# A first part whose weights, vectors, taps and x are laid out by the host

## The chip, the cores and the metric

The kernel runs on one core of a Trainium2 chip. The metric is the device time of one execution in microseconds; before the change the median of three runs is 2349.42 us (2344.43 to 2352.29). The core has five engines that run side by side and meet at semaphores: PE (TensorE, matmuls and transposes, with its weight loads listed as PEld), DVE (VectorE), ACT (ScalarE), POOL (GpSimd) and SP (SyncE, which here only issues DMAs). Sixteen DMA engines move data between HBM and the on-chip memory (SBUF, 128 partitions). Matmul results go to PSUM.

## The reference

A decoder trunk of two layers on x of 256 tokens by 2048 features in float32. Layer 0 mixes tokens by a Conformer convolution module, layer 1 by differential attention; each layer ends with a squared-ReLU MLP. All is modulated by a vector c through six vectors per layer (shift, scale and gate for the mixer and for the MLP):

```python
cond = jax.nn.silu(c)
mod = cond @ ada_w[i] + ada_b[i]
sh_m, sc_m, g_m, sh_f, sc_f, g_f = [m[:, None, :] for m in jnp.split(mod, 6, axis=-1)]
h = x * (1.0 + sc_m) + sh_m
# layer 0
u = h @ w1 + b1
a, gt = jnp.split(u, 2, axis=-1)
u = a * jax.nn.sigmoid(gt)
u = depthwise_causal_conv(u, w_dw, width=31) + b_dw
y = jax.nn.silu(layer_norm(u, g, b)) @ w2 + b2
# every layer
x = layer_norm(DEEPNORM_ALPHA * x + g_m * y, ln_mix_g[i], ln_mix_b[i])
h = x * (1.0 + sc_f) + sh_f
y = jnp.square(jax.nn.relu(h @ mlp_w1 + mlp_b1)) @ mlp_w2 + mlp_b2
x = layer_norm(DEEPNORM_ALPHA * x + g_f * y, ln_ffn_g[i], ln_ffn_b[i])
```

## The kernel before

Every product with weights is made of three matmuls: a weight and an activation are each split into a high part (a cast to fp32r, on ACT) and a low part (the rest, a subtraction on DVE), and high by high, low by high and high by low are summed in PSUM (L580 to L582 in the first part, L669 to L672 in the rest). A weight block is 1 MB, 128 partitions by 2048 columns (`w_pw` or `w_w`); its two halves are split one after the other into `wh` and `wl` (L568 and L569, L629 and L631).

The first part, to which the change is confined, runs from the start to the second pointwise product of the convolution module, some 465 us in. It computes h and its first product (pw1, 2048 by 4096) while the modulation vectors are still being made. The 16 blocks of 128 features are taken in six slices (`SLICES`: 1, 1, 2, 4, 4, 4). For each slice the scale and shift are computed first (the ada weights of the slice, 32-column matmuls on PE, L327 and L290, or multiply-adds on DVE, L249), then h of the slice is made, and then PE takes the slice's share of pw1 for eight groups of output columns, with the sums kept in SBUF (`sums`, `vtok`, L1118 to L1122). While PE works on a slice, the ada work of the next one runs between its matmuls. Behind the last slice come the gated unit, the depthwise convolution on PE (`cv`, L896), and the remaining modulation vectors of layer 0.

Weights and vectors are read as the reference holds them:

- An ada block is a strip of 128 to 1024 columns out of rows of 12288, for 2 to 16 row blocks (L208 to L220, L306 to L321). A row of a piece is 512 bytes in the first slices and 1, 2 or 4 KB later. For the first three slices scale and shift stand side by side in one block, which takes two loads.
- A pw1 block is loaded as two halves (the value columns and the gate columns), with rows of 4 KB or 2 KB (L549 to L559).
- x is read with tokens on partitions into `z`, in four pieces (`X_AT`). For h it must have features on partitions: PE transposes it (`h_t`, L508 and L1090), DVE and ACT read the transposed block from PSUM, multiply and add (`h_h`, L517, L520, L1095), and then split it (`h_hi`, `h_lo`). For two blocks at a time both read one PSUM tile; DVE makes one, ACT the other. When two pairs of a slice are done, ACT multiplies z in place by ALPHA (L1080), eight times in all, since the residual of the layer needs ALPHA times x.
- Small vectors (c, biases, layer norm factors) are read as rows of 128 (`rows_c`, `rows_adab`, `small_rows`, 18 loads), transposed on PE and copied to SBUF as columns (`as_cols`, L129 to L137). The taps of the depthwise convolution are transposed too and spread into `wct` by 4 copies on DVE and 12 on ACT (L976, L978).

The order of PE is written out for the whole program, that of DVE, ACT and SP for the first part (`manual_schedule`); each engine takes its instructions in that order. SP issues every load except one. It waits until the buffer is free and until one of eight semaphores is (a load reuses that of the eighth load before it). The buffers of ada blocks are reused in turn (`ada_raw`: two of their own, and pieces of `conv_ux` and `conv_x` that the convolution needs later); the four of pw1 blocks are `raw`.

Of the kernel before, what the change touches and what calls it, by code (L numbers as in the profile page):

```python
# [76 lines left out]

@with_exitstack
def trunk(
# [41 lines left out]
    def load_rows(rows_list, name, queue=None):  # L121

        rt = work.tile([P, P], F32, tag="S", name=f"rows_{name}", bufs=3)
        o = 0
        for r in rows_list:
            (queue or nc.scalar).dma_start(rt[o:o + r.shape[0], :], r)
            o += r.shape[0]
        return rt[:o, :]

    def as_cols(rt, name):  # L130

        n = rt.shape[0]
        pt = tp_tile(f"pt_{name}")
        nc.tensor.transpose(out=pt[:, :n], in_=rt, identity=ident[:n, :n])
        ct = const.tile([P, n], F32, name=f"cols_{name}")
        nc.vector.tensor_copy(ct, pt[:, :n])
        return ct  # L137

    def vec_rows(v):
        return v.rearrange("(n p) -> n p", p=P)  # L140
# [5 lines left out]
    taps = work.tile([P, NG], F32, tag="C", name="taps")[:4 * CW]  # L146
    small_rows = {}
    rows_sb = work.tile([P, NG], F32, tag="bc_b2", name="small_rows", bufs=1)

    def load_small(n, name, vs):  # L150
        o = 0
        for v in vs:
            r = vec_rows(v)
            nc.sync.dma_start(rows_sb[o:o + r.shape[0], n * P:(n + 1) * P], r)
            o += r.shape[0]
        small_rows[name] = rows_sb[:o, n * P:(n + 1) * P]

    cT = as_cols(c_rows, "c")
# [51 lines left out]
    def slice_tiles(i, v, f0, nf):  # L210

        n0, w = (v * KC + f0) * P, nf * P
        per = 2048 // w
        av = ada_w[i].rearrange("(kc p) n -> p kc n", p=P)

        def load(a):
            t = ada_raw(f"aw_{i}_{v}_{f0}_{a}")
# [1 line left out]
            nc.sync.dma_start(tv, av[:, per * a:per * (a + 1), n0:n0 + w])
# [84 lines left out]
    def ada_both_steps(i, f0, nf, ms):  # L304
# [6 lines left out]
        av = ada_w[i].rearrange("(kc p) n -> p kc n", p=P)  # L311

        def load(b, k=None):
            t = ada_raw(f"aw_{i}_b{k}_{f0}_{b}")
            tv = t.rearrange("p (j n) -> p j n", n=wt)
            for n, (v, _) in enumerate(ms):
                if k in (None, n):
                    n0 = (v * KC + f0) * P
# [1 line left out]
                    nc.sync.dma_start(tv[:, :, o:o + w], av[:, per * b:per * (b + 1), n0:n0 + w])  # L320
# [178 lines left out]
    def to_featT(src, pair, mul, add, name, c2s):  # L499


        pts = {}
        for c2 in c2s:
            pts[c2] = tp_tile(f"{name}_t{c2}")
            for j in range(2):
                cc = 2 * c2 + j
                for t in range(NT):
                    nc.tensor.transpose(out=pts[c2][:, j * S + t * P: j * S + (t + 1) * P],  # L508
                                        in_=src[:, t, cc * P:(cc + 1) * P], identity=ident)

# [589 lines left out]
    def put_h(s, c2, now=True):  # L1100
# [10 lines left out]
        if now:  # L1111
            rest()
# [728 lines left out]
```

## Time and profile before

| | |
|---|---|
| median of three runs | 2349.42 us (2344.43 to 2352.29) |
| span of the profiled execution, first to last instruction | 2342.9 us |
| instructions | 28838 |
| moved by DMA | 606.5 MB, mean 259 GB/s |
| mean granted clock of TensorE | 0.995 |
| matmuls of pw1 (L580 to L582) | 768 |
| ada blocks of layer 0 in the first part | 88 MB (5.25 of 6 vectors) |

The page gives no time of the profiled execution outside its span. In the views below a row of a timeline holds the start in us, the duration in us, the engine, the line, the operation, the tile it writes and the tiles it reads, the shape, a count and, in brackets, the idle time before it with what ended it. SPq and ACTq are issues of DMAs. A row of the groups holds the count, then the busy time in us with the mean of one in ns, and the idle time before. Matmul durations overlap, since PE is pipelined; what a matmul costs in a row of others is the distance between starts.

### The profile page before, as it was taken

The numbers are of one execution on the slowest core, as the hardware profiler recorded it, in microseconds if no ns is written. First come the engines' busy times: TensorE is split into PE (matmuls) and PEld (weight loads), VectorE is DVE, ScalarE is ACT, GpSimd is POOL, SyncE is SP. The second block draws the span as 40 slices with busy tenths as digits, with TensorE's granted clock in tenths as the row PEclk, the third lists the DMA queues.
The fourth block names the chain that finished last, engine by engine and source line by source line (L and its number), as shares of the span: only waits on it lengthen the run. The fifth ranks groups of instructions, "written<-read, shape, count | busy, mean of one in ns | idle before, by whom it ended". The sixth has DMA issues, their size and how long they took to land.

```text
span 2342.9 us, 28838 instructions
## 1 busy us (share of the span) xinstructions
PE 2279.1 (97%) x11265; PEld 1809.2 (77%) x11265; DVE 1743.6 (74%) x2031; ACT 1089.7 (47%) x1503; POOL 149.4 (6%) x110
## 2 busy tenths in 40 slices
PE   7999989999999999999999999999999999999999
PEld 4676647777788888888878888877888888888886
DVE  5787788878887888877878876887975655655566
ACT  3344674365345445445454454545443443443442
POOL 0000002002200000000004200010220000000000
PEclk9999999999999999999999999999999999999999
DMA  9998489869988888888847655784876565555563
GB/s 342 377 341 295 164 314 376 316 221 329 326 315 308 312 290 307 308 301 291 310 163 269 242 201 195 256 319 162 305 247 202 180 197 191 187 186 193 189 223 108
DMA packets 264721, 606.50 MB, mean 259 GB/s; under 512 B 11137, under 2 KB 24583, under 8 KB 251527
## 3 DMA queue, kind: packets, MB, share of 16 engines
q1 hardware_dynamic: 264472, 604.62, 73.9%
q8 instruction: 88, 1.44, 0.3%
q14 instruction: 49, 0.39, 0.0%
q10 hardware_dynamic: 112, 0.05, 0.0%
HBM read 602.48 MB, written 2.15 MB: 258 GB/s over the span
## 4 chain that ended last, share of the span: by engine, by line
PE 74%; issue 16%; DVE 6%; ACT 2%; DMA 2%; POOL 0%; POOLq 0%; ACTq 0%; DVEq 0%; SPq 0%
PE w_ps L669 18%; PE w_ps L671 18%; PE w_ps L672 18%; DVE wl_w L631 1%; DMA w_w<-in_mlp_w_dram 1%; PE pw_ps L669 1%; PE qkv_v_ps L672 1%; PE qkv_v_ps L669 1%; PE qkv_v_ps L671 1%; PE qkv_q_ps L672 1%; PE qkv_q_ps L669 1%; DVE acc L379 1%; PE qkv_q_ps L671 1%; PE pw_ps L671 1%; PE pw_ps L672 1%
## 5 line engine op out<-in xcount | busy, mean ns | idle before, releaser
L631 DVE TENSOR_TENSOR wl_w<-w_w,wh_w 128x1024 fp32r<-128x1024 f32 x510 | 633.3, 1259 | 340.0 <-ACT wh_w L629 339.3
L629 ACT CAST wh_w<-w_w 128x1024 fp32r<-128x1024 f32 x512 | 537.0, 1054 | 703.4 <-PE w_ps L672 563.9
L669 PE MATMUL w_ps<-wh_w,hm_hi 128*128 128x512 f32 x1024 | 402.3, 393 | 3.0 <-ACT hm_hi L490 3.0
L671 PE MATMUL w_ps<-wl_w,u_hi 128*128 128x512 f32 x1024 | 399.4, 390 | 4.1 <-DVE wl_w L631 4.1
L671 PE MATMUL w_ps<-wl_w,hm_hi 128*128 128x512 f32 x1024 | 399.5, 390 | 2.5 <-DVE wl_w L631 2.5
L672 PE MATMUL w_ps<-wh_w,hm_lo 128*128 128x512 f32 x1024 | 399.3, 390 | 1.6 <-DVE hm_lo L493 1.6
L669 PE MATMUL w_ps<-wh_w,u_hi 128*128 128x512 f32 x1024 | 400.6, 391 | 0.0
L672 PE MATMUL w_ps<-wh_w,u_lo 128*128 128x512 f32 x1024 | 399.1, 390 | 0.0
L379 DVE SCALAR_TENSOR_TENSOR acc<-adaw,cond,acc 128x2048 f32<-128x2048 f32 (+1 forms) x105 | 244.5, 2329 | 0.1
L669 PEld LDWEIGHTS w_ps<-wh_w,hm_hi 128*128 128x128 f32 x1024 | 192.5, 188 | 47.5 <-ACT hm_hi L490 4.5
L671 PEld LDWEIGHTS w_ps<-wl_w,u_hi 128*128 128x128 f32 x1024 | 192.4, 188 | 45.3 <-DVE wl_w L631 5.8
L671 PEld LDWEIGHTS w_ps<-wl_w,hm_hi 128*128 128x128 f32 x1024 | 192.5, 188 | 43.4 <-DVE wl_w L631 4.6
L672 PEld LDWEIGHTS w_ps<-wh_w,hm_lo 128*128 128x128 f32 x1024 | 192.4, 188 | 43.0 <-DVE hm_lo L493 3.1
L669 PEld LDWEIGHTS w_ps<-wh_w,u_hi 128*128 128x128 f32 x1024 | 192.6, 188 | 42.0 <-issue 1.7
L672 PEld LDWEIGHTS w_ps<-wh_w,u_lo 128*128 128x128 f32 x1024 | 192.5, 188 | 40.2
L580 PE MATMUL pw_ps<-wh_pw,h_hi 128*128 128x512 f32 x256 | 105.7, 413 | 9.4 <-DVE sums L1122 3.3
L581 PE MATMUL pw_ps<-wl_pw,h_hi 128*128 128x512 f32 x256 | 101.5, 397 | 5.1 <-DVE wl_pw L569 5.1
L582 PE MATMUL pw_ps<-wh_pw,h_lo 128*128 128x512 f32 x256 | 100.8, 394 | 0.0
L569 DVE TENSOR_TENSOR wl_pw<-w_pw,wh_pw 128x1024 fp32r<-128x1024 f32 x64 | 77.5, 1220 | 21.2 <-ACT wh_pw L568 21.2
L568 ACT CAST wh_pw<-w_pw 128x1024 fp32r<-128x1024 f32 x64 | 65.8, 1050 | 41.6 <-PE pw_ps L582 24.5
L580 PEld LDWEIGHTS pw_ps<-wh_pw,h_hi 128*128 128x128 f32 x256 | 48.5, 190 | 39.5 <-issue 16.1
L581 PEld LDWEIGHTS pw_ps<-wl_pw,h_hi 128*128 128x128 f32 x256 | 48.7, 190 | 15.9 <-DVE wl_pw L569 7.2
(375 smaller groups left out, 3147.4 us busy)
## 6 DMA issues: line engine op xcount, KB each, us to landing
w_w<-in_mlp_w_dram SPq DMA_DIRECT2D x256, 1024.0 KB, 5.4
adaw<-in_ada_w_dram SPq DMA_DIRECT2D x96, 1024.0 KB, 5.6
aw<-in_ada_w_dram SPq DMA_DIRECT2D x40, 1024.0 KB, 7.3
w_pw<-in_conv_pw_w_dram SPq DMA_DIRECT2D x64, 512.0 KB, 9.1
conv_ux<-in_ada_w_dram SPq DMA_DIRECT2D x17, 1024.0 KB, 12.9
w_pw<-in_conv_pw_w_dram SPq DMA_DIRECT2D x16, 1024.0 KB, 9.2
w_qkv_q<-in_attn_qkv_w_dram SPq DMA_DIRECT2D x16, 1024.0 KB, 5.4
w_qkv_k<-in_attn_qkv_w_dram SPq DMA_DIRECT2D x16, 1024.0 KB, 5.2
```

Of the source, the lines that this page charges most:

```text
L379: nc.vector.scalar_tensor_tensor(st["acc"], w, cond[:, kc:kc + 1], st["acc"], ALU.mult, ALU.add)
L568: nc.scalar.copy(hq, rq)
L569: nc.vector.tensor_tensor(lq, rq, hq.bitcast(F32), op=ALU.subtract)
L580: nc.tensor.matmul(pss[t], lhsT=xh, rhs=wh, start=(kc == first), stop=False)
L581: nc.tensor.matmul(pss[t], lhsT=xh, rhs=wl, start=False, stop=False)
L582: nc.tensor.matmul(pss[t], lhsT=xl, rhs=wh, start=False, stop=(kc == last))
L629: nc.scalar.copy(hi, rq)
L631: eng.tensor_tensor(lo, rq, hi.bitcast(F32), op=ALU.subtract)
L669: nc.tensor.matmul(pss[tt], lhsT=xh, rhs=wh, start=(kc == 0 and job["bias"] is None), stop=False)
L671: nc.tensor.matmul(pss[tt], lhsT=xh, rhs=wl, start=False, stop=False)
L672: nc.tensor.matmul(pss[tt], lhsT=xl, rhs=wh, start=False, stop=(kc == nk - 1))
```

## The change

The host makes six new inputs (`lay_out`), and the first part reads them:

```diff
+def ada_specs():
+    out = []
+    for s, (f0, nf) in enumerate(SLICES):
+        if s < BOTH_PE and 2 * nf * P <= NG:
+            out += [("both", f0, nf, a) for a in range(2 * nf)]
+        else:
+            out += [(v, f0, nf, a) for v in (SC_M, SH_M) for a in range(nf)]
...
+def lay_out(inputs):
...
+        ada.append(aw[per * a:per * (a + 1), :, vs, f0:f0 + nf, :].transpose(1, 0, 2, 3, 4).reshape(P, 2048))
...
+    pw1 = [pw[c0:c0 + nk, :, :, g:g + ng].transpose(1, 0, 2, 3, 4).reshape(P, 2048)
+           for _, c0, nk, g, ng in pw1_specs()]
...
+        "x_t": i["x"][0].T.reshape(KC, P, S).transpose(1, 0, 2),
+        "taps_t": taps, "ada_tiles": np.stack(ada), "pw1_tiles": np.stack(pw1),
...
-    c_rows = load_rows([vec_rows(c[0])], "c", nc.sync)
-    adab0_rows = load_rows([vec_rows(ada_b[0])], "adab0")
+    vec0 = const.tile([P, KC + 6 * KC], F32, name="vec0")
+    nc.scalar.dma_start(vec0, cols_first)
+    vec1 = const.tile([P, cols_rest.shape[1]], F32, name="vec1")
...
+    xT = z.rearrange("p t (a n) -> p (t a) n", n=S)
...
             t = ada_raw(f"aw_{i}_{v}_{f0}_{a}")
-            tv = t.rearrange("p (j n) -> p j n", n=w)
-            nc.sync.dma_start(tv, av[:, per * a:per * (a + 1), n0:n0 + w])
-            return tv
+            nc.sync.dma_start(t, ada_tiles[ADA_AT[v, f0, nf, a]])
+            return t.rearrange("p (j n) -> p j n", n=w)
...
-                    nc.tensor.transpose(out=pts[c2][:, j * S + t * P: j * S + (t + 1) * P],
-                                        in_=src[:, t, cc * P:(cc + 1) * P], identity=ident)
...
+    def chunk_h(mul, add, c0, n):
+        h32 = [work.tile([P, 1, S], F32, tag="B", name=f"h0_h{c0 + j}") for j in range(n)]
+        for j in range(n):
+            cc = c0 + j
+            if j == 0:
+                nc.vector.tensor_scalar(h32[j][:, 0, :], xT[:, cc, :], mul[:, cc:cc + 1], add[:, cc:cc + 1],
+                                        ALU.mult, ALU.add)
+            else:
+                nc.scalar.activation(h32[j][:, 0, :], xT[:, cc, :], AF.Identity,
+                                     scale=mul[:, cc:cc + 1], bias=add[:, cc:cc + 1])
+        for j in range(n):
+            put_split(hT, c0 + j, 1, 0, S, h32[j])
...
-        for h in range(2):
-            raws["dma"] = nc.sync.dma_start(rv[:, :, h, :], src[:, :, h, :])
+        raws["dma"] = nc.sync.dma_start(raw, pw1_tiles[n])
...
         nc.vector.tensor_tensor(tmp, ps, gb[:, sl], op=ALU.mult)
-        nc.vector.tensor_tensor(z[:, t, sl], z[:, t, sl], tmp, op=ALU.add)
+        if times is None:
+            nc.vector.tensor_tensor(z[:, t, sl], z[:, t, sl], tmp, op=ALU.add)
+        else:
+            nc.vector.scalar_tensor_tensor(z[:, t, sl], z[:, t, sl], times, tmp, ALU.mult, ALU.add)
...
-    def alpha_x(q):
-        sl = slice(q * NG, (q + 1) * NG)
-        for t in range(NT):
-            nc.scalar.activation(z[:, t, sl], z[:, t, sl], AF.Copy, scale=ALPHA)
...
             if (s, h) == (3, 0):
-                load_small(0, "conv", [conv_pw1_b[0], conv_dw_b[0], conv_ln_g[0], conv_ln_b[0]])
-                nc.sync.dma_start(taps, conv_dw_w[0].rearrange("k (q c) -> (k q) c", q=4))
...
+                nc.sync.dma_start(vec1, cols_rest)
+                nc.sync.dma_start(wct.rearrange("p a k b -> p (a k b)"), taps_t)
+            elif (s, h) == (5, 9):
+                nc.sync.dma_start(z, x[0].rearrange("(t p) d -> p t d", p=P))
```

- Every ada block of layer 0 and every pw1 block is one load of 128 rows of 8 KB that lie together in HBM, in the order in which the kernel reads them.
- The vectors come as columns in two loads, `vec0` (c and layer 0's ada bias, on ACT's queue) and `vec1` (all others); the taps come as `wct` is used. Their transposes and copies are gone.
- x comes with features on partitions (`xT`, in the place of `z`, in the same four pieces), and h is made from it without a transpose. In slice 5 x is loaded once more, with tokens on partitions, into the same `z`. It isn't scaled by ALPHA there; the gated add of pw2 multiplies by it (`times`).

The order of all other instructions, and that of everything behind the first part, is the same on each engine. On SP the program begins before with (c's rows, ada blocks in halves, a piece of x, pw1 blocks in halves):

```order
L126 DMA rows_c<-in_c_dram 16x128
L320 DMA aw_bNone_0_139<-in_ada_w_dram 128x8x128 x2
L320 DMA aw_bNone_1_142<-in_ada_w_dram 128x8x128 x2
L1127 DMA z<-in_x_dram 128x2x256
L554 DMA w_pw_0_0_0_146<-in_conv_pw_w_dram 128x1024 x2
L554 DMA w_pw_4_0_0_149<-in_conv_pw_w_dram 128x1024 x2
L320 DMA conv_ux<-in_ada_w_dram 128x8x128 x4
```

and after the change with the same blocks, one load each:

```order
L338 DMA aw_bNone_0_132<-in_ada_tiles_dram 128x2048
L338 DMA aw_bNone_1_134<-in_ada_tiles_dram 128x2048
L1070 DMA z<-in_x_t_dram 128x512
L558 DMA w_pw_0_0_0_137<-in_pw_tiles_dram 128x2048
L558 DMA w_pw_4_0_0_139<-in_pw_tiles_dram 128x2048
L338 DMA conv_ux<-in_ada_tiles_dram 128x2048 x2
```

The blocks stand in the same order; c's load is no longer ahead of them.

On ACT, at the boundary to slice 2, before (one of two h blocks, the two casts, z's scaling, weight casts; brackets hold the semaphores that a row waits for):

```order
L520 ACTIVATE h_h_476<-h_t_454,mod_0_128,h_mul 128x256 [waits DVE_49,PE_49,Activation_49]
L490 CAST h_hi<-h_h_475 128x256
L490 CAST h_hi<-h_h_476 128x256 [waits Activation_49]
L1080 ACTIVATE z<-z 128x512 [waits DMAHW6_49,DMAHW1_49]
L1080 ACTIVATE z<-z 128x512
L568 CAST wh_pw_0_2_0_1_507<-w_pw_0_2_0_303 128x1024
```

and after:

```order
L526 ACTIVATE h_h_438<-z,mod_0_121,h_mul 128x256 [waits DMAHW5_49,DVE_49,Activation_49]
L508 CAST h_hi<-h_h_437 128x256 [waits DVE_49]
L508 CAST h_hi<-h_h_438 128x256 [waits Activation_49]
L572 CAST wh_pw_0_2_0_1_467<-w_pw_0_2_0_277 128x1024
L572 CAST wh_pw_2_2_0_0_486<-w_pw_2_2_0_279 128x1024 [waits DMAHW0_49,PE_49]
```

The two rows of scaling are gone, and the wait for DVE's block has moved from ACT's own h to the cast of DVE's h.

On SP, towards the end of slice 5, before (ada blocks of the vectors that are needed later):

```order
L219 DMA aw_2_8_3_1847<-in_ada_w_dram 128x4x512
L219 DMA aw_2_0_5_1901<-in_ada_w_dram 128x2x1024
L219 DMA aw_2_12_0_2010<-in_ada_w_dram 128x4x512
L219 DMA aw_2_0_6_2012<-in_ada_w_dram 128x2x1024
L219 DMA aw_2_12_1_2014<-in_ada_w_dram 128x4x512
```

and after:

```order
L243 DMA aw_2_8_3_1690<-in_ada_tiles_dram 128x2048
L243 DMA aw_2_0_5_1744<-in_ada_tiles_dram 128x2048
L1150 DMA z<-in_x_dram 128x2x2048
L243 DMA aw_2_12_0_1854<-in_ada_tiles_dram 128x2048
L243 DMA aw_2_0_6_1856<-in_ada_tiles_dram 128x2048
L243 DMA aw_2_12_1_1858<-in_ada_tiles_dram 128x2048
```

The load of x with tokens on partitions has come in, as one load of 2 MB.

More of the change, by code (lines that the diff above doesn't have):

```diff
@@ L119, in inv_sqrt @@
         nc.gpsimd.tensor_tensor(dst, src, neg_half.broadcast_to([P, n]), op=ALU.pow)
[L121 to L140, printed above, removed]
-    c_rows = load_rows([vec_rows(c[0])], "c", nc.sync)
-    adab0_rows = load_rows([vec_rows(ada_b[0])], "adab0")
-    vtok = big.tile([P, NT, D], F32, tag="uTl", name="vtok")
[L146 to L158, printed above, removed]
+    vec0 = const.tile([P, KC + 6 * KC], F32, name="vec0")
+    nc.scalar.dma_start(vec0, cols_first)
+    vec1 = const.tile([P, cols_rest.shape[1]], F32, name="vec1")
+    vtok = big.tile([P, NT, D], F32, tag="uTl", name="vtok")
+    cT = vec0[:, :KC]
     cond = const.tile([P, KC], F32, name="cond")
@@ L834, in base_bias, with add_gated @@
             defer(step * (q + 1), lambda q=q: quarter(q))
[L836 removed]
+    def add_gated(ps, gb, t, q, name, times=None):
         sl = slice(q * NG, (q + 1) * NG)
@@ L1084, in end_ada, with put_h @@
             f()
[L1086 to L1113 removed]
+    def put_h(s, c2):
+        f0, nf = SLICES[s]
+        c0, n = (f0, 1) if nf == 1 else (2 * c2, 2)
+        if c0 == f0:
+            nc.vector.tensor_scalar(mul[:, f0:f0 + nf], m_sc[:, f0:f0 + nf], 1.0, None, ALU.add)
+        chunk_h(mul, m_sh, c0, n)
     def add_up(g, s, pss):
@@ L1222, in trunk @@
                 split_half(s)
-            if s == 3 and 5 <= h < 9:
-                tap_columns(h - 5)
-            elif (s, h) == (3, 9):
-                conv_vectors()
+            if (s, h) == (3, 5):
+                nc.vector.tensor_reduce(eye, ident.rearrange("p (r c) -> p c r", c=32), axis=AX.X, op=ALU.add)
             if h in PAIR_AT[s]:
@@ L1335, in ln_t, with out_proj @@
         return [stats, norm]
-    def out_proj(pair, w2d, gate, name, pump, at_end, start=None, hold=False, on_pool=((),) * 4, bias=None):
+    def out_proj(pair, w2d, gate, name, pump, at_end, start=None, hold=False, on_pool=((),) * 4, bias=None,
+                 times=None):
         st = stats_tile(name)
@@ L1385, in trunk @@
     out_proj(lambda: oT, conv_pw2_w[0], gate0, "pw2", pump_t2, lambda st, t: ln_t(st, t, ALPHA, "lnm0"),
-             start=early_ve.__enter__, on_pool=POOL_T2,
+             start=early_ve.__enter__, on_pool=POOL_T2, times=ALPHA,
              bias=lambda q: lambda: [(bias0["one"][:, q:q + 1].broadcast_to([4, P]), bias0["hl"][:, n, :])
```

157 lines of the change are left out of this document (49 added, 108 removed).

## The prediction

> **What bounds the kernel now.** I read the page's head first, then the windows by stage, then the PE timeline of the first 260 us, since the change touches only that part.
>
> ```profile
> span 2342.9 us, 28838 instructions
> PE 2279.1 (97%) x11265; PEld 1809.2 (77%) x11265; DVE 1743.6 (74%) x2031; ACT 1089.7 (47%) x1503; POOL 149.4 (6%) x110
> ```
>
> PE is busy for 97% of the span. Matmul times overlap in this view, so that is not the last word, but it leaves at most some tens of microseconds of waits. Where they lie is seen by stage (columns: the busy time of PE, PEld, DVE, ACT and POOL with instructions, the granted clock, the DMA share, GB/s):
>
> ```profile
> 0.00:20.00 20.00, 8.16 (x43) 4.22 (x44) 5.58 (x14) 5.63 (x9) 2.02 (x12) 1.00 0.97 289
> 20.00:140.00 120.00, 111.26 (x576) 77.17 (x576) 87.91 (x137) 47.67 (x72) 0.00 (x0) 1.00 1.05 375
> 140.00:260.00 120.00, 114.04 (x665) 84.00 (x667) 96.85 (x142) 57.40 (x81) 0.00 (x0) 1.00 0.71 256
> 460.00:2342.00 1882.00, 1854.98 (x8405) 1516.14 (x8403) 1380.83 (x1485) 871.93 (x1180) 130.31 (x91) 1.00 0.71 244
> ```
>
> The reader is to see three stages. Until 140 us the DMA engines are full (shares 0.97 and 1.05) and PE has 20.6 us without work. From 140 to 260 the DMA has room (0.71) and PE lacks 6 us. From 460 on PE is short of 27 us in 1882; nothing there is touched, and the order of the instructions there is the same, so that part should only start earlier. So the first part has two bounds that lie close together: PE, and until 140 us the transfers.
>
> How fast the transfers go depends on the length of a row. The same view, in stretches in which the queue is full and nearly all pieces are alike: 512 bytes (2 to 10 us), 4 KB (24 to 28), 2 KB (60 to 68), half 8 KB (364 to 368), and layer 1's 8 KB rows among 2 KB ones (596 to 600, 700 to 712):
>
> ```profile
> 2.00:10.00 8.00, 2.55 (x18) 1.05 (x18) 0.94 (x4) 0.67 (x2) 0.58 (x3) 1.00 1.06 273
> 24.00:28.00 4.00, 4.00 (x37) 2.81 (x39) 2.07 (x3) 0.71 (x2) 0.00 (x0) 1.00 1.02 406
> 60.00:68.00 8.00, 8.00 (x49) 4.45 (x42) 4.64 (x6) 1.41 (x2) 0.00 (x0) 1.00 1.05 387
> 364.00:368.00 4.00, 4.00 (x30) 3.60 (x29) 1.00 (x2) 2.89 (x6) 0.00 (x0) 1.00 1.01 398
> 596.00:600.00 4.00, 4.00 (x19) 3.30 (x19) 0.00 (x0) 2.08 (x2) 0.00 (x0) 1.00 1.01 405
> 700.00:712.00 12.00, 12.00 (x58) 10.00 (x57) 9.42 (x7) 5.82 (x7) 0.00 (x0) 1.00 1.00 361
> ```
>
> So 512-byte rows cost a third of the rate (273 against 387 to 406), and from 2 KB on there is little left to win: 2 to 5%.
>
> **The start (edit 1: whole blocks, and c as a column).** The timelines of SP, PE and ACT:
>
> ```profile
> 1.17 4.18 SPq L320 DMA_DIRECT2D aw_bNone<-in_ada_w_dram  x4
> 7.45 1.94 PE L327 MATMUL aps_b<-aw_bNone,condr 128*32 128x256 f32 x16 [4.34 <-DMA aw_bNone<-in_ada_w_dram]
> 11.04 1.94 PE L327 MATMUL aps_b<-aw_bNone,condr 128*32 128x256 f32 x16 [1.65 <-DMA aw_bNone<-in_ada_w_dram]
> 15.88 2.93 ACT L568 CAST wh_pw<-w_pw 128x1024 fp32r<-128x1024 f32 x3
> 16.97 0.79 PE L580 MATMUL pw_ps<-wh_pw,h_hi 128*128 128x512 f32 x1 [2.39 <-ACT wh_pw L568]
> ```
>
> PE waits for the first 2 MB of ada weights; the second MB lands at about 10.9 us, 9.7 after the first issue at 1.17. 2.1 MB at 273 GB/s are 7.7 us, so 2.0 are latency. In the change SP issues these loads first, at about 0.7 (c's row load leaves SP), and 2.1 MB at 403 GB/s (the mean of 406, 398 and 405; the 361 is kept for the range) are 5.2 us: landed at 0.7 + 2.0 + 5.2 = 7.9, 3.0 us sooner. From there to the first conv matmul at 16.97 the chain stays (PE, ACT, PE, DVE, ACT); x and the first conv block follow in the queue (1.3 MB, 3.3 us, landed at 11.2), before ACT casts it at 15.88 - 3.0 = 12.9. With 0.1 from a shorter step in it: **3.1 us**; bounds 2.4 (at 361 GB/s) and 3.7 (less latency).
>
> **PE work that goes (edit 2: x, taps and vectors come with features on partitions).**
>
> ```profile
> 30.18 0.38 PE L1090 MATMUL h_t<-ident,z 128*128 128x128 f32 x2
> 30.40 0.38 PE L353 MATMUL apt_b<-ident,arow_b 128*128 128x128 f32 x2
> ```
>
> Two transposes hold PE for 0.22 us, so 0.11 each (the 0.38 is pipelined). 32 transposes of x go, of which the first 2 lie in the start's chain, and 9 for taps and vectors after the start. Until 140 us that is 14 + 5, **2.0 us**; from 140 to 260 it is 16 + 4, **2.2 us**. PE is the engine that is waited for in these places, so they count in full. The copies out of PSUM that go with them are small work of DVE and ACT.
>
> **Slice boundaries (edit 3: h is made from SBUF, and ACT no longer scales z by ALPHA).** The timelines of DVE and ACT at the boundary to slice 2:
>
> ```profile
> 50.50 0.54 DVE L517 TENSOR_SCALAR h_h<-h_t,h_mul,mod 128x256 f32<-128x256 f32 x1
> 52.05 0.76 DVE L493 TENSOR_TENSOR h_lo<-h_h,h_hi 128x256 fp32r<-128x256 f32 x2 [1.00 <-ACT h_hi L490]
> 51.16 0.56 ACT L520 ACTIVATE h_h<-h_t,mod,h_mul 128x256 f32<-128x256 f32 x1 [3.48 <-DVE h_h L517]
> 51.62 0.70 ACT L490 CAST h_hi<-h_h 128x256 fp32r<-128x256 f32 x2
> 52.22 1.15 ACT L1080 ACTIVATE z<-z 128x512 f32<-128x512 f32 x2
> 53.55 0.47 PE L580 MATMUL pw_ps<-wh_pw,h_hi 128*128 128x512 f32 x1 [2.27 <-DVE sums L1122]
> ```
>
> Both halves of a pair read one PSUM tile, and ACT starts its half only when DVE has ended its own (51.04, then 51.16). In the change ACT's half waits only for the factor, and the order rows show a wait of its own for the first cast; so both halves run beside each other, 0.6 us sooner per pair. DVE's own half shortens too:
>
> ```profile
> L247 DVE TENSOR_SCALAR aacc<-aw,cond 128x512 f32<-128x512 f32 x2 | 1.0, 480 | 0.0
> L517 DVE TENSOR_SCALAR h_h<-h_t,h_mul,mod 128x256 f32<-128x256 f32 x7 | 3.8, 542 | 3.3 <-PE h_t L508 3.2
> ```
>
> From SBUF twice the columns take 480 ns, from PSUM half take 542, so some 0.2 us more go. And four times 1.15 us of scaling leave ACT just ahead of a weight cast. There are 7 pairs. What counts are the waits of PE behind them: the 2.27 us at 53.55, and at the next three boundaries
>
> ```profile
> 88.72 0.50 PE L580 MATMUL pw_ps<-wh_pw,h_hi 128*128 128x512 f32 x1 [1.13 <-ACT h_hi L490]
> 93.44 0.50 PE L581 MATMUL pw_ps<-wl_pw,h_hi 128*128 128x512 f32 x1 [0.76 <-DVE wl_pw L569]
> 148.22 0.50 PE L581 MATMUL pw_ps<-wl_pw,h_hi 128*128 128x512 f32 x1 [1.66 <-DVE wl_pw L569]
> 206.24 0.50 PE L581 MATMUL pw_ps<-wl_pw,h_hi 128*128 128x512 f32 x1 [1.17 <-DVE wl_pw L569]
> ```
>
> These are 4.2 us until 140 and 2.8 after it. I take two thirds, **2.8 and 1.9 us**, since each wait follows one or two pairs of 0.8 us and a scaling; the bounds for both together are 1 (the DVE work between them sets the pace anyway) and 7 (all goes). The scaling comes back on DVE as a multiply inside the gated add, which takes a third operand:
>
> ```profile
> L249 DVE SCALAR_TENSOR_TENSOR aacc<-aw,cond,aacc 128x512 f32<-128x512 f32 x18 | 13.5, 750 | 0.4
> L840 DVE TENSOR_TENSOR z<-z,pw_g 128x512 f32<-128x512 f32 x7 | 4.8, 693 | 0.2
> ```
>
> That is 0.06 us eight times before 465 us; most of it lies beside PE's matmuls, and I count **0.2 us** lost for the last ones, ahead of the layer norm.
>
> **Transfers until 140 us.** Waits of PE that end with a DMA:
>
> ```profile
> 71.44 1.06 PE L327 MATMUL apsb<-conv_ux,condr 128*32 128x512 f32 x8 [1.49 <-DMA conv_ux<-in_ada_w_dram]
> 126.46 1.07 PE L290 MATMUL aps<-conv_ux,condr 128*32 128x512 f32 x8 [1.47 <-DMA conv_ux<-in_ada_w_dram]
> 360.47 1.08 PE L290 MATMUL aps<-aw,condr 128*32 128x512 f32 x4 [2.46 <-DMA aw<-in_ada_w_dram]
> ```
>
> The first two, **3.0 us**, go if the loads run ahead (bounds: none and both). The third stays: its load is issued when a buffer comes free, and rows of 4 KB become 8 KB there. By PE's side the stage gains 3.1 + 2.0 + 2.8 + 3.0 = 10.9 us. PE can't get ahead of its loads either: 289 x 20 + 375 x 120 is 50.8 MB by 140 us, and 50.8 MB at 403 GB/s from 2.7 us on (0.7 + 2.0) end at 128.8, 11.2 us sooner. The smaller one counts: **10.9 us**, and the two bounds now lie together.
>
> **The second load of x.** 2 MB, some 5.2 us, stand on SP between two ada loads: by the timeline of SP three of these are issued from 230.1 to 244.6 us (230.12 + 14.52), and x goes ahead of the last. The windows show that the queue is empty before it:
>
> ```profile
> 230.12 14.52 SPq L219 DMA_DIRECT2D aw<-in_ada_w_dram  x3
> ...
> 238.00:244.00 6.00, 6.00 (x64) 4.08 (x53) 5.79 (x10) 4.13 (x7) 0.00 (x0) 1.00 0.01 3
> ```
>
> It costs nothing there; without that gap the ada loads behind it would come 5 us later.
>
> **The sum.** 10.9 + 2.2 + 1.9 - 0.2 = 14.8 us off the span of 2342.9, so 2328.1. The three runs have a median of 2349.4, 6.5 above this span, for what lies around it and for their spread; that stays. Forecast 2349.4 - 14.8 = 2334.6, given as **2335**. One per cent is 23 us; a change under 0.3%, about 7 us, can't be told from none by a measurement of this kernel.
>
> **Rivals.** *Rows longer than 2 KB win nothing* (387 GB/s throughout, as at 60 to 68): the loads of the first 140 us then end at 134.0, 6.0 us sooner, and with the 3.9 won after it the time is 2339.5. For it: the small step from 387 to 398. Against: 406. *DVE takes over*: it is busy for 96.9 of 120 us from 140 to 260, so a PE that is early only waits there; the 3.9 go, and 3 of the lead, a gain of 8 and 2341. Against it: in that stage DVE itself waits,
>
> ```profile
> L569 DVE TENSOR_TENSOR wl_pw<-w_pw,wh_pw 128x1024 fp32r<-128x1024 f32 x31 | 37.7, 1221 | 11.2 <-ACT wh_pw L568 11.1
> ```
>
> so it has 11 us of its own to give. *Whole blocks move no faster than the mix of 700 to 712* (361): the loads end at 143.4, 3.4 late, less 3.9: 2349, no change.
>
> *The other side*: 16 engines reading one packed block get in each other's way, so that the full queue moves at less than pieces taken from long rows do. The place is 2 to 140 us. It decides from 343 GB/s down: 50.8 MB then end at 150.8, 10.8 us late, against 3.9 won later, which is 7 us slower. At the lowest full-queue rate of these rows, 273, they would end at 188.8, 48.8 late, and the time would be 2394. For it speaks that no row shows whole packed blocks, and the 361 at a full share; against it, that stretches with 8 KB rows also reach 398 and 405.
>
> [...]
>
> **How the numbers follow.** Forecast 0.62; no gain over 2 KB 0.16; DVE takes over 0.12; 361 or the like 0.06; slower 0.04. Bounds of the terms: least is 2.4 + 4.2 + 1 with no DMA wait gone, 7.6, so 2342; most is 3.7 + 4.2 + 7 + 3.0 and the third DMA wait's 2.5, 20.4, so 2329. With 3 us on each side, since the runs lie 3 to 5 from their median: 2326 to 2345, which leaves out the last two cases. Faster by over 0.3%: the forecast and the first rival, and half of DVE's: 0.84. Within 0.3%: the other half and the 361: 0.12. Slower: 0.04.
>
> **What would show it.** First conv matmul near 13.9 us; DMA rate near 400 GB/s in 2 to 100 us with no wait for a DMA at 71 and 126; the boundary's two h halves starting together; the conv phase's first products and everything behind it some 15 us sooner, and the stretch from 460 us on as long as before (1882). Wrong would be: a rate under 380 with shares above 1, PE waits that name wl_pw in 100 to 260 us grown, or ada loads late after 240 us.

## The result, and the profile after

The changed kernel takes 2336.21 us (median of four runs, 2332.89 to 2338.70) where the kernel before takes 2350.68 beside it (four runs): a ratio of 0.9945, 95% interval 0.9929 to 0.9961, about 13 us less. Run again later with five runs it gave 2334.96 us and 0.9945 (0.9932 to 0.9958). The forecast was 2335, in a range of 2326 to 2345.

The page's head, and the windows by stage and by stretches in which the queue is full (columns as before):

```profile
span 2331.1 us, 28624 instructions
PE 2273.9 (98%) x11222; PEld 1805.5 (77%) x11222; DVE 1739.4 (75%) x2020; ACT 1082.5 (46%) x1483; POOL 147.6 (6%) x109
```

```profile
0.00:20.00 20.00, 9.39 (x47) 5.37 (x48) 7.31 (x15) 7.23 (x10) 1.51 (x11) 1.00 0.92 368
20.00:140.00 120.00, 114.70 (x590) 79.49 (x588) 92.74 (x143) 45.41 (x61) 0.00 (x0) 1.00 0.98 398
140.00:260.00 120.00, 115.64 (x744) 84.20 (x737) 98.95 (x152) 56.34 (x79) 0.00 (x0) 1.00 0.70 272
...
2.00:10.00 8.00, 3.06 (x32) 1.33 (x32) 0.60 (x2) 0.65 (x2) 0.08 (x1) 1.00 0.94 374
10.00:40.00 30.00, 25.05 (x134) 16.61 (x127) 21.06 (x38) 13.53 (x20) 0.00 (x0) 1.00 1.01 421
100.00:120.00 20.00, 20.00 (x97) 14.69 (x95) 16.50 (x22) 5.46 (x7) 0.00 (x0) 1.00 1.01 421
```

Whole blocks move at 421 GB/s with the queue full, above the 403 that the sum used and the 387 of 2 KB rows. That settles three of the four rivals: rows over 2 KB do win something, the rate isn't that of the mix at 361, and packed blocks move no slower than pieces of long rows did before (421 after 398 to 406). The fourth rival, DVE, has become no bound either: PE is busy for 115.64 of the 120 us from 140 on, 1.6 more than before, and from slice 4 to the last product of pw1 it takes 4.5 us less (table below).

The start, in the timeline:

```profile
0.71 0.40 ACTq L180 DMA_DIRECT2D vec<-in_cols_first_dram  x1
0.72 0.86 SPq L338 DMA_DIRECT2D aw_bNone<-in_ada_tiles_dram  x2
6.01 0.21 ACT L185 ACTIVATE cond<-vec 128x16 f32<-128x16 f32 x1 [3.58 <-DMA vec<-in_cols_first_dram]
6.95 3.64 PE L345 MATMUL aps_b<-aw_bNone,condr 128*32 128x256 f32 x32 [6.95 <-DVE condr L189]
14.44 0.79 PE L584 MATMUL pw_ps<-wh_pw,h_hi 128*128 128x512 f32 x1 [2.61 <-ACT wh_pw L572]
```

The first product of pw1 comes at 14.44 in place of 16.97. PE now waits for c at the start, not for the first ada block. The boundary to slice 2 and the next one:

```profile
47.21 0.41 DVE L523 TENSOR_SCALAR h_h<-z,h_mul,mod 128x256 f32<-128x256 f32 x1
47.26 0.60 ACT L526 ACTIVATE h_h<-z,mod,h_mul 128x256 f32<-128x256 f32 x1 [2.56 <-issue]
49.69 0.47 PE L584 MATMUL pw_ps<-wh_pw,h_hi 128*128 128x512 f32 x1 [1.84 <-DVE sums L1066]
...
82.52 0.50 PE L584 MATMUL pw_ps<-wh_pw,h_hi 128*128 128x512 f32 x1 [1.42 <-ACT h_hi L508]
86.77 0.50 PE L585 MATMUL pw_ps<-wl_pw,h_hi 128*128 128x512 f32 x1 [0.76 <-DVE wl_pw L573]
```

The two halves of h start together here (47.21 and 47.26), and yet PE's waits have hardly changed: 1.84 us after 2.27, 1.42 after 1.13, 0.76 after 0.76. What is gone entirely are the waits for DMAs at 71 and 126 us and the wait of 1.66 at the first products of slice 4. In five of the seven pairs the halves start within 0.12 us of each other. In the second pairs of slices 4 and 5 ACT goes further ahead, by 2.46 and 4.39 us; the first of these:

```profile
129.47 0.59 ACT L526 ACTIVATE h_h<-z,mod,h_mul 128x256 f32<-128x256 f32 x1
131.93 0.41 DVE L523 TENSOR_SCALAR h_h<-z,h_mul,mod 128x256 f32<-128x256 f32 x1
```

Further on, the second load of x and the third wait for an ada block:

```profile
217.13 0.43 SPq L1150 DMA_DIRECT2D z<-in_x_dram  x1
230.07 0.33 SPq L243 DMA_DIRECT2D aw<-in_ada_tiles_dram  x1
...
345.55 1.07 PE L314 MATMUL aps<-aw,condr 128*32 128x512 f32 x8 [1.41 <-DMA aw<-in_ada_tiles_dram]
```

SP waits 12.5 us behind the load of x (217.56 to 230.07), for a buffer that PE's ada products free, no wait of PE follows from it, and from 234 to 246 us the queue is empty as before.

Where the gain came from is best read from the starts of the same products in the traces (us; "behind" is the time from the first product of the MLP to the end):

```
                     before   again    after   repeat
first of pw1          17.0     17.3     14.4     14.5
first of slice 4     143.5    142.6    133.8    133.8
last of pw1          269.9    269.2    255.6    255.5
last of pw2          460.5    459.8    444.2    444.3
first of the MLP     468.1    467.2    452.4    452.4
end                 2342.9   2346.0   2331.1   2332.9
behind              1874.9   1878.8   1878.6   1880.5
```

"again" and "repeat" are second profiles of the unaltered kernels (below). In these pairs the first part repeats within 1 us, and it is some 15 us shorter. The untouched rest differs by 2 to 4 us between two executions of one kernel.

The distance from each product of pw1 to the next, before less after, put down to what lies between the two, splits the 11.7 us won between the first and the last product of pw1:

```
                                  to slice 4    behind
transposes of x (22, 8)              2.4          0.9
9 transposes of taps and vectors     0.6          0.7
waits for a DMA                      3.2          0
other waits (wh, wl, h, sums)        0.5          2.7
others                               0.4          0.2
```

A transpose makes 0.11 us of it, as the prediction had it.

### The profile page after: what moved, and what is told of

The parts are those of the page before. It is cut to its first block, busy times and chain, and to the rows that moved or that the text cites. A ratio compares the mean times of both kernels' runs of the same rounds, so it can differ in the third digit from the quotient of the medians.

```text
span 2331.1 us, 28624 instructions
## 1 busy us (share of the span) xinstructions
PE 2273.9 (98%) x11222; PEld 1805.5 (77%) x11222; DVE 1739.4 (75%) x2020; ACT 1082.5 (46%) x1483; POOL 147.6 (6%) x109
## 4 chain that ended last, share of the span: by engine, by line
PE 74%; issue 15%; DVE 6%; DMA 2%; ACT 2%; POOL 0%; POOLq 0%; SPq 0%; DVEq 0%; ACTq 0%
PE w_ps L675 18%; PE w_ps L676 18%; PE w_ps L673 18%; DMA w_w<-in_mlp_w_dram 2%; DVE wl_w L635 1%; PE pw_ps L673 1%; PE qkv_v_ps L676 1%; PE qkv_v_ps L673 1%; PE qkv_v_ps L675 1%; DVE acc L397 1%; PE qkv_q_ps L676 1%; PE qkv_q_ps L673 1%; PE qkv_q_ps L675 1%; PE pw_ps L676 1%; PE pw_ps L675 1%
## 5 line engine op out<-in xcount | busy, mean ns | idle before, releaser
L675 PEld LDWEIGHTS w_ps<-wl_w,u_hi 128*128 128x128 f32 x1024 | 192.7, 188 | 46.2 <-DVE wl_w L635 6.4
L572 ACT CAST wh_pw<-w_pw 128x1024 fp32r<-128x1024 f32 x64 | 65.5, 1050 | 51.6 <-PE pw_ps L586 38.7
L584 PEld LDWEIGHTS pw_ps<-wh_pw,h_hi 128*128 128x128 f32 x256 | 48.4, 189 | 38.9 <-issue 13.9
L633 ACT CAST wh_pw<-w_pw 128x1024 fp32r<-128x1024 f32 x32 | 33.5, 1052 | 58.4 <-PE pw_ps L676 54.7
```

Source lines behind the costliest of these rows:

```text
L572: nc.scalar.copy(hq, rq)
L584: nc.tensor.matmul(pss[t], lhsT=xh, rhs=wh, start=(kc == first), stop=False)
L633: nc.scalar.copy(hi, rq)
L675: nc.tensor.matmul(pss[tt], lhsT=xh, rhs=wl, start=False, stop=False)
```

## The experiments

Medians and ratios to the kernel before, with what the traces give for the first product of the MLP:

| kernel | median us (runs) | ratio (95%) | MLP starts |
|---|---|---|---|
| weights_only | 2345.54 (12) | 0.9985 (0.9975 to 0.9995) | 461.5 |
| x_vec_only | 2340.85 (8) | 0.9970 (0.9960 to 0.9981) | 461.4 |
| before_again | 2347.82 (1) | none | 467.2 |
| repeat | 2334.96 (5) | 0.9945 (0.9932 to 0.9958) | 452.4 |
| idle_t | 2335.84 (5) | 0.9941 (0.9925 to 0.9956) | 453.6 |
| scale_x | 2338.04 (6) | 0.9947 (0.9928 to 0.9965) | 454.8 |
| serial_h | 2344.87 (7) | 0.9972 (0.9961 to 0.9982) | 460.7 |
| keep_busy | 2335.68 (5) | 0.9945 (0.9930 to 0.9960) | 452.4 |
| mlp_packed | 2331.95 (5) | 0.9934 (0.9919 to 0.9948) | 453.2 |
| gate_only | 2334.73 (6) | 0.9937 (0.9920 to 0.9953) | 454.8 |
| packed_gate | 2329.08 (4) | 0.9907 (0.9892 to 0.9922) | 453.6 |

### Half of the change each

weights_only is the kernel before with the new block loads alone:

```diff
-                    nc.sync.dma_start(tv[:, :, o:o + w], av[:, per * b:per * (b + 1), n0:n0 + w])
+            nc.sync.dma_start(t, ada_tiles[ADA_AT["both" if k is None else ms[k][0], f0, nf, b]])
...
-            raws["dma"] = nc.sync.dma_start(rv[:, :, h, :], src[:, :, h, :])
+        raws["dma"] = nc.sync.dma_start(raw, pw1_tiles[n])
```

> Ada and pw1 blocks laid out as whole 1 MB blocks; x, vectors and taps as before (transposes, scaling by ALPHA and copies stay). Theory A (each term has one cause, and the terms add): the start (2.5 us), the two waits of PE for a DMA at 71 and 126 us (3.2) and most of the third at 360 (2.4) go, about 8.1 us in all: last product of pw2 at 452.4 in place of 460.5, time 0.9966 of before. The transposes stay at 0.14 us each and the wait at 148 us stays. Theory B (the transfers were the bound of the first 140 us, and PE's own work only sat beside them): almost everything comes with the weights, 14 us or more, time 0.994. Theory C (weights give nothing without the rest): under 3 us, time 0.999 or more.

x_vec_only is the changed kernel with these lines the other way round.

> x with features on partitions, vectors and taps as columns; ada and pw1 blocks read as before (strips of 512 bytes to 4 KB, halves). Theory A (terms add): 6.1 us of transposes and about 2.9 at slice boundaries go, start as before; the waits for DMAs at 71, 126 and 360 us stay as they are; about 9 us, last product of pw2 at 451.5, time 0.996. Theory B (PE can't get ahead of its loads): what PE saves until 140 us (about 4.3) comes back as longer waits for DMAs at 71 and 126 us, since the queue is full at 375 GB/s; only what is saved after 140 us stays, 4 to 5 us, and the waits at 71 and 126 together grow from 3.2 to 7; time 0.998.

Neither half brings nearly all of it: 3.5 and 7.0 us by the ratios, where both together bring 12.9. In the trace of weights_only the two waits for DMAs at 71 and 126 us are gone; the wait at slice 4 is still there, and so is most of the third wait for an ada block, which theory A had mostly gone:

```profile
51.58 0.76 PE L618 MATMUL pw_ps<-wh_pw,h_hi 128*128 128x512 f32 x1 [2.24 <-DVE sums L1160]
...
144.49 0.50 PE L619 MATMUL pw_ps<-wl_pw,h_hi 128*128 128x512 f32 x1 [1.66 <-DVE wl_pw L607]
...
354.81 1.56 PE L335 MATMUL aps<-aw,condr 128*32 128x512 f32 x8 [2.04 <-DMA aw<-in_ada_tiles_dram]
...
51.50:54.90 3.40, 3.32 (x8) 2.68 (x9) 3.40 (x5) 2.72 (x3) 0.00 (x0) 0.50 1.02 419
```

The row of the window shows PE at half clock (granted clock 0.50) behind the wait at 51.58, which the profile before hasn't there; it takes 1.7 us off what the loads bring (8 products in 3.4 us, where the changed kernel has 15 in the 3.41 us from 49.60 on). So theory A's 8.1 us show as 6.5 at the MLP, and by the median as still less; why the median keeps so little of it isn't settled. The profiled executions of weights_only and x_vec_only (2350.08 and 2350.47 us) are the slowest of their kernels, so they tell little of the part behind the MLP's start. In x_vec_only PE's waits for DMAs are:

```profile
64.09 1.06 PE L354 MATMUL apsb<-aw_b,condr 128*32 128x512 f32 x8 [1.22 <-DMA aw_b<-in_ada_w_dram]
70.79 1.07 PE L354 MATMUL apsb<-conv_ux,condr 128*32 128x512 f32 x8 [1.70 <-DMA conv_ux<-in_ada_w_dram]
...
123.13 1.06 PE L316 MATMUL aps<-conv_ux,condr 128*32 128x512 f32 x8 [0.52 <-DMA conv_ux<-in_ada_w_dram]
...
351.91 1.93 PE L316 MATMUL aps<-aw,condr 128*32 128x512 f32 x8 [2.63 <-DMA aw<-in_ada_w_dram]
```

That is 6.1 us in four, after 5.4 in three. PE is 4.3 us early at slice 4 and 8.8 at the last of pw1, as theory A has it; the old loads didn't hold it back: its waits for DMAs until 140 us come to 3.4 us, after 3.0 (theory B expected 7). 2.1 us of the 8.8 are lost again until the MLP starts, most of them at half clock, which lasts 6.8 us from 351.4 on, where the kernel before has 3.4 from 360.0 on. The load of `vec0` is that of the changed kernel, issued at 0.71 too, but beside rows of 512 bytes c can be used 3.2 us sooner (2.77, not 6.01):

```profile
2.77 0.22 ACT L185 ACTIVATE cond<-vec 128x16 f32<-128x16 f32 x1 [0.31 <-DMA vec<-in_cols_first_dram]
```

### Which part of the PE side

idle_t puts the 32 transposes back where they were, with nothing reading them:

```diff
+        pt = tp_tile(f"idle_t{c0}")
+        for j in range(n):
+            for t in range(NT):
+                nc.tensor.transpose(out=pt[:, j * S + t * P: j * S + (t + 1) * P],
+                                    in_=xT[:, c0 + j, t * P:(t + 1) * P], identity=ident)
```

> The changed kernel with the 32 transposes of x put back on PE at the places where the kernel before had them; nothing reads what they write. Theory A (PE is what is waited for there): 0.14 us each, 3.1 us more until the first product of slice 4 and 1.1 more until the last of pw1; last product of pw2 at 448.5 in place of 444.2, time 0.9963 of before. Theory B (they fall into waits of PE that are there anyway, at slice boundaries above all): less than 2 us in all, time 0.995.

From the first product of slice 1 to the last of pw1, past the half clock of the start (products 0.43 us apart until 18.8 us in the changed kernel, 0.23 from 19.1 on), the changed kernel takes 224.2 us (224.0 in its second profile) and this one 226.2. The 28 transposes in it hold PE for 3.1 us (0.11 each, by the distances between products) and cost 2.0: a third falls into waits that are there anyway. The boundary to slice 3 shows it:

```profile
81.84 0.60 PE L1057 MATMUL idle_t<-ident,z 128*128 128x128 f32 x4
82.94 0.50 PE L584 MATMUL pw_ps<-wh_pw,h_hi 128*128 128x512 f32 x1 [0.51 <-ACT h_hi L508]
```

PE is at the first product of the slice 0.4 us later than in the changed kernel (82.52), as it was at the slice before (50.13 after 49.69). The four transposes cost nothing here: the wait behind them has shrunk from 1.42 to 0.51. By the cost theory B is nearer, and in the time (0.9941) nothing can be seen. The 0.14 us of theory A counted in the 0.23 us of the product ahead of each group, which that product takes in any case.

scale_x puts the scaling back on ACT, in place, by 1.0:

```diff
+            v = xT[:, 4 * q + 2 * t:4 * q + 2 * t + 2, :]
+            nc.scalar.activation(v, v, AF.Copy, scale=1.0)
```

> The changed kernel with eight in-place scalings of x (by 1.0, 128x512 each, 1.15 us) put back on ACT where the kernel before scaled z by ALPHA. Theory A (the scalings, ahead of weight casts, made the wait of PE for wl_pw at the first products of slice 4): that wait of 1.8 us is back near 138 us, and the boundary at 49.7 grows by 0.3; last product of pw2 2 us later, at 446.3. Theory B (the wait went because both halves of h now run beside each other): no wait above 1 us near 138, last product of pw2 within 0.5 of 444.2. What I forecast for both together was 2.8 us until 140 us and 1.9 behind it; the rows of the changed kernel show 0.4 and 2.5.

(One scaling takes 0.62 us; 1.15 is a pair.) Theory B: no wait near 138 us. Between the first of pw1 and slice 4 it takes 1.8 us more, and one stretch has nearly all of it:

```profile
46.80:50.21 3.41, 1.56 (x8) 1.02 (x7) 2.81 (x7) 2.62 (x6) 0.00 (x0) 1.00 1.02 423
50.21:53.62 3.41, 3.41 (x9) 2.66 (x9) 3.41 (x5) 2.47 (x3) 0.00 (x0) 0.50 1.02 418
```

The changed kernel, at the same place:

```profile
46.18:49.60 3.42, 1.67 (x8) 1.05 (x6) 2.82 (x7) 2.34 (x5) 0.00 (x0) 1.00 1.01 419
49.60:53.01 3.41, 3.32 (x15) 2.76 (x16) 3.41 (x5) 1.99 (x3) 0.00 (x0) 1.00 1.02 418
```

The wait in front is the same (1.85 and 1.84), but here 9 products run in the stretch behind it, there 15: half clock (0.50) for 3.41 us costs 1.7. What is left for the scaling is 0.1. mlp_packed (below) confirms it: its first part is that of the changed kernel, without scalings, it has the same half clock from 50.21 on, and it takes 121.0 us from the first product of pw1 to slice 4, where scale_x takes 121.1. The last product of pw2 comes at 447.4, 3.2 us late and not within 0.5 as theory B has it: these 1.7 us are in it, and half clock again from 347.2 on, behind the third wait for an ada block.

serial_h makes ACT's half wait for DVE's again, by seven more short steps on DVE:

```diff
+                m2 = small.tile([P, 1], F32, tag="m2", name=f"m2_{cc}")
+                nc.vector.scalar_tensor_tensor(m2, h32[0][:, 0, 0:1], 0.0, mul[:, cc:cc + 1], ALU.mult, ALU.add)
                 nc.scalar.activation(h32[j][:, 0, :], xT[:, cc, :], AF.Identity,
-                                     scale=mul[:, cc:cc + 1], bias=add[:, cc:cc + 1])
+                                     scale=m2, bias=add[:, cc:cc + 1])
```

> The changed kernel, but ACT's half of each pair of h blocks waits again for DVE's half: its factor is written by a short DVE step (about 0.06 us) that reads the end of DVE's half. h is still made from SBUF, without transposes. Theory A (the halves beside each other took the wait for wl_pw off slice 4): the wait of 1.8 us is back near 138 us, the boundaries at 49.7 and 82.5 grow by about 0.6 each, last product of pw2 2.5 to 3 us later than in the changed kernel (444.2). Theory B (it went because h comes from SBUF and DVE has fewer copies to make, or because the transposes are gone): no wait above 1 us near 138; the first part within 1 us of the changed kernel's. Time 0.9945 to 0.9957 of before, too close for the times to tell; the trace decides.

```profile
47.87 0.41 DVE L523 TENSOR_SCALAR h_h<-z,h_mul,mod 128x256 f32<-128x256 f32 x1
48.32 0.16 DVE L527 SCALAR_TENSOR_TENSOR m<-h_h,h_mul 128x1 f32<-128x1 f32 x1
48.56 0.60 ACT L528 ACTIVATE h_h<-z,mod,m 128x256 f32<-128x256 f32 x1 [3.20 <-issue]
...
50.99 0.47 PE L586 MATMUL pw_ps<-wh_pw,h_hi 128*128 128x512 f32 x1 [2.44 <-DVE sums L1068]
...
86.08 0.50 PE L586 MATMUL pw_ps<-wh_pw,h_hi 128*128 128x512 f32 x1 [2.04 <-ACT h_hi L508]
...
142.19 0.50 PE L587 MATMUL pw_ps<-wl_pw,h_hi 128*128 128x512 f32 x1 [1.27 <-DVE wl_pw L575]
```

Theory A, and this time the runs see it too: 0.9972 lies outside the changed kernel's intervals, 6.3 us lost by the ratios. ACT starts 0.69 us behind DVE (0.66 before the change), and not only where the halves started together: in the two pairs in which ACT was 2.46 and 4.39 us ahead it is now 0.70 behind. The waits at both boundaries grow by 0.6, and a wait for wl_pw of 1.27 is back at slice 4, where the changed kernel has none. From the first product of slice 1 to the last of pw1 it takes 229.3 us after 224.2, 5.1 more. 1.7 of these are half clock at 51.5 us, which scale_x and mlp_packed have too, behind waits of 1.85 and 1.80 us; so 3.4 belong to the halves themselves. The seven steps on DVE take 0.16 us each, 1.1 in all, not the 0.06 each that was expected and that no run shows; how much of the 3.4 they make isn't shown. Further on more is lost: the last product of pw2 comes at 454.1, 9.9 us late and not 2.5 to 3, with a third wait for an ada block of 2.36 us after 1.41 and half clock behind it.

### What the untouched rest does

The kernels of the next two runs are unaltered.

> The changed kernel once more, unaltered. What is asked: the profiled run lost 3.7 us more than before between the first product of the MLP of layer 0 (452.4) and the end, in instructions that weren't touched. Theory N (chance of one execution: where a load lands among others, and where the 3 to 4 us of half clock after a wait of PE fall): the stretch from that product to the end differs from 1878.7 by 1 us or more in this second profile. Theory S (a start that is 15 us earlier meets the loads of the MLP in a worse order): it is 1878.7 within 0.5 again, with the wait of 1.7 us near 524 and half clock at 596 to 599. Time 0.9945 of before, within 0.993 to 0.996.

> The kernel before once more, unaltered, for a second profile of it. Theory N (the profiled execution of before was a lucky one behind 468 us): its first part comes out as before (first product of the MLP at 468.1, within 1.5), and the 1000 products of layer 0's MLP that follow take 2 to 5 us longer than the 250.4 us of the first profile, about as long as the 253.4 to 259.0 of the four kernels with another first part. Theory S (an earlier start makes that stretch longer): 250.4 again, within 1.

The 1000 products that follow the first of the MLP took 253.4 us in the changed kernel's first profile and 254.6 in its second, the time from there to the end 1878.6 and 1880.5: theory N by its own mark, since they differ by 1.8. Before (2347.82 us in its one run) took 250.4 and 251.8 for the 1000, between the marks of the two theories, and 1874.9 and 1878.8 to the end. idle_t, which has the changed loads, took 250.1, scale_x 255.2. So a single execution is good to some 2 to 4 us here, and whether an earlier start costs some 2 us on average stays open.

mlp_packed also lays the MLP blocks of layer 0 out as whole blocks:

```diff
+        "w1_tiles": i["mlp_w1"][0].reshape(4, 4, P, 16, NG).transpose(3, 0, 2, 1, 4).reshape(16, 4, P, 2048),
+        "w2_tiles": i["mlp_w2"][0].reshape(4, 4, 4, P, 4, NG).transpose(0, 4, 1, 3, 2, 5).reshape(4, 4, 4, P, 2048),
```

> The changed kernel, with the weight blocks of layer 0's MLP (both products) laid out as whole 1 MB blocks too; everything else as in the changed kernel. Theory A (PE's waits for wl_w between 490 and 600 us come from transfers that run at 300 to 346 GB/s with the queue full): at about 400 GB/s the waits at 493, 517, 524 and 543 (4.1 us) go, and perhaps some of 590 and 596; 4 to 6 us less than the changed kernel, time 0.992 of before. Theory B (those loads are issued late, when a buffer comes free, so that their rate doesn't matter): under 1.5 us, time 0.994 to 0.9945, and the waits stay.

Its median is 3 us lower, its interval overlaps the changed kernel's, and its 1000 products take 253.5 us. The waits ahead of these come to 8.2 us, after 8.6 and 7.8 in the two profiles of the changed kernel, so they stay, as theory B has it. Two large ones stand 5 us apart, and it isn't the blocks' loads that they wait for:

```profile
590.87 0.50 PE L677 MATMUL w_ps<-wl_w,u_hi 128*128 128x512 f32 x1 [1.86 <-DVE wl_w L637]
596.38 0.79 PE L677 MATMUL w_ps<-wl_w,u_hi 128*128 128x512 f32 x1 [2.49 <-DVE wl_w L637]
```

Ahead of them DVE waits for the gate's trip through HBM. packed_gate starts that trip one step earlier, gate_only does the same without the MLP's new blocks:

```diff
-                defer(5, start_gate)
+                defer(4 if i == 0 else 5, start_gate)
```

> The kernel with the MLP blocks of layer 0 as whole blocks, and the gate of that MLP made one step (some 2.7 us of products) earlier, since its trip through HBM (two transfers of 7 us in a full queue) makes DVE wait 5.4 us before the first gated add, and PE then waits 2.0 and 2.7 us for wl_w at 591 and 596. Theory A: DVE's wait falls by about 2.7 us and PE's two waits by 2 to 3 us in all; time 0.992 of before. Theory B (DVE is behind with other work there): PE's two waits stay at 4 to 5 us, time 0.9934 as without it.

> The changed kernel with one edit alone: the gate of layer 0's MLP is made one step earlier; MLP blocks are read as in the changed kernel (2 KB rows). Theory A (the gate's early start is what took PE's waits near 591 and 596 away, the layout of the MLP blocks did little): 1000 products from the first of the MLP in 248 to 251 us in place of 253.4 and 254.6, time 0.992 of before. Theory B (both edits are needed, as whole blocks let the gate's two transfers through sooner): under 1 us less than the changed kernel, time 0.9940 to 0.9945.

The first row is of mlp_packed, the second of packed_gate:

```profile
586.80 0.69 DVE L848 TENSOR_TENSOR w2g<-w_ps,gbm 128x512 f32<-128x512 f32 x1 [6.12 <-DMA gbm<-gbm_d]
```

```profile
582.11 0.69 DVE L848 TENSOR_TENSOR w2g<-w_ps,gbm 128x512 f32<-128x512 f32 x1 [0.72 <-DMA gbm<-gbm_d]
```

DVE's wait falls from 6.1 to 0.7 us (1.1 in gate_only) and PE's two waits are gone; a new one of 2.1 us, for the vector itself, stands ahead of the gate. In the ten profiles with neither this edit nor added work in these waits the two come to 3.4 to 5.2 us, in both with the edit to nothing. The 1000 products take 248.0 us, with the gate alone 250.9, about what idle_t took without it. packed_gate is the fastest kernel of this study: its interval, 0.9892 to 0.9922, lies below that of the changed kernel. For gate_only the times can't tell.

### The half clock

keep_busy adds transposes that nothing reads where PE waits:

```diff
+                        if tt == 0 and key == "w2_0_0_1" and kc in (6, 8):
+                            keep_busy(12, f"{key}_{kc}")
                         nc.tensor.matmul(pss[tt], lhsT=xh, rhs=wl, start=False, stop=False)
+                        if tt == 0 and key in ("qkv_q0", "w1_1_0_0") and kc == 0:
+                            keep_busy(8, key)
```

> The changed kernel with 40 more transposes on PE that nothing reads, in four places behind 585 us where PE waits 1.6 to 2.5 us: 12 each ahead of the two waits for wl_w in the second block group of layer 0's second MLP product (590 and 595 us in the changed kernel), 8 each in the first products of the attention (1197) and of layer 1's MLP (1598). In six profiles, behind the first 22 us, every stretch of 3.41 us (on a fixed grid) with PE busy for 0.47 of it or less was followed by 3.41 us at half clock, and with two exceptions none with 0.5 or more before the last 25 us. Theory A (the idle share of a stretch sets the clock of the next): no half clock at 595, 1197 and 1599 any more; the products from 585 us to the end come 1.5 to 4 us sooner than in the changed kernel, time 0.9935 of before. Theory B (half clock comes from something else, as the load behind the wait): episodes as before, and the time is that of the changed kernel or up to 2 us above it.

The changed kernel around 595 us, and then keep_busy:

```profile
592.30:595.70 3.40, 0.91 (x5) 0.45 (x4) 3.40 (x3) 1.04 (x1) 2.10 (x1) 1.00 0.84 278
595.70:599.10 3.40, 3.40 (x9) 2.62 (x10) 3.40 (x4) 0.00 (x0) 0.00 (x0) 0.50 1.08 406
```

```profile
592.70:596.20 3.50, 3.12 (x15) 2.58 (x16) 3.50 (x2) 0.31 (x2) 3.50 (x2) 1.00 0.63 194
596.20:599.60 3.40, 2.22 (x16) 1.84 (x14) 3.40 (x4) 0.76 (x1) 1.26 (x1) 1.00 0.83 285
```

The half clock is gone at 595, 1197 and 1599, as theory A says, and another came at 1610. (At 1197 the second profile of the changed kernel has none either, so there it could be chance.) In this run PE is busy for 0.65 and 0.66 of the 3.41 us from 596.5 and from 1596.6 with the transposes, and would be for 0.39 and 0.40 without them; full clock follows both, where in the profiles before and after half clock followed all nine such stretches at 0.24 to 0.44. So here the transposes count as work. By the starts of the same products it is 3.7 us behind the changed kernel at 585 us and 1.5 at 602. The next 1.2 us, won at 1197, are lost again by 1208, where PE now waits 2.05 us for h in place of 1.71 (as in the second profile of the changed kernel), and at 1610 it is the same (2.05 after 1.47), with half clock behind it. At the end it is 2.7 us behind: 1.0 is won where theory A had 1.5 to 4, and the time is the changed kernel's. What the filling takes away at one wait, the next brings back here.

## Why the prediction came out, step by step

- **The start**, 3.1 us: 2.5. The second ada block landed at 8.35 in place of 7.9, since the first stretch ran at 374 GB/s, not 403. And c, in a load on ACT's queue beside the 8 KB rows, let PE begin only at 6.95; from there its 32 products ran without a wait, so that c, to which the sum gave nothing, set the pace.
- **Transposes**, 2.0 and 2.2 us: the price of 0.11 us holds, and all 39 held PE for 4.6 us. They were put in the wrong places: 18 of x, not 14, stand ahead of 140 us, and 22 ahead of slice 4. And "PE is the engine that is waited for in these places, so they count in full" was wrong for a third of the time: put back, 28 of those of x cost 2.0 us of the 3.1 they hold. The other nine weren't put back.
- **Slice boundaries**, 2.8 and 1.9 us: 3.4 by serial_h, and it is the two halves side by side that make them. The scaling makes 0.1, and the waits at 53.55 and 88.72 that I counted on for the first 2.8 are still there, at 1.84 and 1.42 us; with the transposes back, in idle_t, they are 1.66 and 0.51. Nor do the halves only run beside each other: in two pairs ACT's goes well ahead, which the prediction didn't foresee. The multiply in the gated add, 0.2 us, cost nothing: it takes 692 ns where the add took 693.
- **The waits for DMAs** at 71 and 126 us, 3.0: 3.2 are gone. That PE "can't get ahead of its loads either" was wrong, since x_vec_only did, with the old loads; nothing of the result rested on it.
- **The third wait stays**: it does, at 1.41 us after 2.46. Behind it the kernel before ran at half clock from 360.0 on, the changed kernel didn't, and the lead grew from 13.9 to 16.3 us there. scale_x, mlp_packed and packed_gate, with the same loads, have the half clock at 347, 347 and 346: part of these 2.4 us is chance.
- **The second load of x** cost nothing, though it went out at 217.13, some 13 us ahead of the three ada loads from 230 on, and not ahead of the last of them as the prediction had it; it had landed by 229.4, before the first of the three was issued.
- **From 460 us on as long as before**: 3.8 us longer in the first profile, -0.2 to 5.6 by pairs of the four profiles. The gain of the first part, 15.6 where 14.8 were forecast, hid this: 11.8 remained in the span.

So the forecast came within 1.2 us of the time (2335 and 2336.2), and that it is so close is luck in part: three terms were too high by what the runs show (start, transposes, boundaries), a gain at the third wait was not foreseen, and a loss behind it may be chance. Of the 11.2 us won between the first product of slice 1 and the last of pw1 the runs account for 8.7: 3.4 for the halves, 3.2 for the waits for DMAs, 2.0 for the transposes of x and 0.1 for the scaling.

## What to carry to other kernels

Ask of two engines that share a job whether one waits for the other: here ACT's half, where it had to wait for DVE's, came 0.6 us later in five pairs and 3.2 and 5.1 us later in two, and that cost 3.4 us, more than the 2.0 of 28 transposes. Work taken off an engine is worth its time only where no wait stands behind it (28 transposes hold PE for 3.1 us here and cost 2.0); putting the same work back as a dead copy measures this. Single profiles of this kernel differ by 2 to 4 us in parts that weren't touched, so compare the starts of the same instruction part by part, and leave the end to the medians.
